# A convolution through DRAM in one step of a hybrid decoder: a smaller trip, the sample columns on VectorE, and the statistics moved into the next stage

## Chip, cores, metric

One Trainium2 chip, eight cores, every core running the same program on its share of the tokens. There is no exchange between cores. The metric is the device time of the slowest core in microseconds. Some executions fall into a second, slower state in which the cores of one die have a lower granted TensorE clock; times and ratios below use fast runs alone.

## The reference, cut to what matters

```python
def decoder_layer(x, ...):
    x = x + 0.5 * swiglu_ffn(rms_norm(x, ffn1_norm), ffn1_w_gu, ffn1_w_down)
    mix, v_state, conv_state = token_mixer(rms_norm(x, mix_norm), ...)
    x = x + mix
    return x + 0.5 * swiglu_ffn(rms_norm(x, ffn2_norm), ...), v_state, conv_state

def token_mixer(h, conv_prev, ...):
    ua, va, glu_a, glu_b, gate_a, gate_b = jnp.split(h @ w_in, SPLITS, axis=-1)
    u = jax.nn.gelu(ua)
    v = layer_norm(jax.nn.gelu(va), ln_v_g, ln_v_b)
    y_a = chunk_spatial_gating(u, v, w_s, b_s) @ w_pa      # u * (W_s v + b_s) per chunk of 128
    g = glu_a * jax.nn.sigmoid(glu_b)
    gpad = jnp.concatenate([conv_prev, g], axis=1)         # 30 earlier rows
    c = depthwise_conv(gpad, w_dw) + b_dw                  # width 31, 2048 channels
    y_b = jax.nn.silu(layer_norm(c, ln_c_g, ln_c_b)) @ w_pb
    m = jax.nn.sigmoid(gate_a) * y_a + jax.nn.sigmoid(gate_b) * y_b
    return m @ w_out, ...
```

Each core has 1024 prompt tokens, 64 sample tokens (16 sequences, 4 tokens each, with 30 cached rows) and 30 halo tokens before its prompt part: 1118 columns, channels on the partitions. The mixer runs as stages: V (for v), GLU with convolution (16 blocks of 128 channels), u (gelu, spatial gating, and beside it the layer norm and silu of the convolution), then gates and branch products.

## The kernel before

`P` is a planner: it records instructions per engine in the order of the Python calls and inserts a semaphore wait wherever a read or write depends on another engine. Each engine runs its list in the order in which it was recorded. `bank()` hands out the eight PSUM banks in turn. The depthwise convolution is a matmul: 32 channels by 4 shifts make the 128 rows, so the GLU result has to be laid out in four shifted copies, and for that it goes through DRAM (`gs_d`, "gspill").

```python
def glu(c):
    g = GBUF[c % 2]
    P.dma("pool", g[:, 1054:1534], cache_d[c])         # cached rows of the samples
    Wt = wk(W.get("glu", c), 256)
    for (c0, n) in S1:                                 # 374, 374, 370 columns
        ...                                            # 2 x 16 matmuls, sigmoid, product into g
    W.done("glu", c)                                   # slot free: starts the next 1 MB weight load
    P.dma("sp", gs_d[c % 2], g, wk=[("gs", c % 2)])    # the whole of g, 1614 columns
    P.dma("sp", gst_o[:, c, :], gf)
    g4 = G4R.get()
    for s in range(4):                                 # four shifts, prompt and samples apart
        P.dma("sp", g4[32*s:32*s+32, :, 0:GPN], src[:, :, s:s + GPN], rk=[("gs", c % 2)])
        P.dma("sp", g4[32*s:32*s+32, :, GPN:G4W], src[:, :, 1054+16*s:1054+16*s+GSN], rk=[("gs", c % 2)])
    ...
def conv(c, g4, dg):
    for (c0, n) in ((0, 512), (512, 512), (1024, 64)): # the third: the samples
        for q in range(8):
            for j in range(4):
                mm(bk[32*j:32*j+32, 0:n], dg[:, q, j, :], rhs, q == 0, q == 7)
        ...                                            # bias, square, running sums SM1, SM2

prev = glu(0)
v_norm()
for c in range(KC):
    nxt = glu(c + 1) if c + 1 < KC else None
    if c == 10:
        W.reserve(4); W.reserve(3)                     # slots kept for BSB and temporaries
    conv(c, *prev)
    prev = nxt
P.dma("sp", BSB..., bsr_d.to_broadcast([128, D]))      # bias table, in the last block's weight slot
...  # statistics of the convolution: 6 f32 matmuls, sqrt, reciprocal, three times in turn
...  # 4 matmuls and 16 VectorE operations that finish BSB
# [cut]
for c in range(KC):                                    # stage u
    for (c0, n) in SU:                                 # 384, 384, 320 columns
        ...                                            # 16 matmuls, 2 to 3 for the gating, gelu
        cn_step()                                      # one step of the convolution's layer norm
        if (c * 3 + SU.index((c0, n))) % 8 == 7:
            cn_step()                                  # subtract DVE, multiply POOL, 2 x ACT, product DVE
```

Of the kernel before, what the change touches and what calls it, by code (L numbers as in the profile page):

```python
# [25 lines left out]
SLOT_B = 8192  # L26
GW = 1054 + 544 + 16
GPN = 1052
GSN = 512
G4W = GPN + GSN  # L30

# [182 lines left out]
def build_program():  # L214
# [10 lines left out]
    pv_d = din("pv", [128, NVEC * 16])  # L225
    wcv_d = din("wcv", [128, 512])
    mask_d = din("mask32", [128, 32])
    maskt_d = din("maskt", [128, 128])
# [17 lines left out]
    xs_d = nc.dram_tensor("xspill", [KC, 128, NM], F32, kind="Internal").ap()  # L246
    gs_d = nc.dram_tensor("gspill", [2, 128, GW], BF16, kind="Internal").ap()

    P = Plan()
    with nc.sbuf_tensor("arena", [128, ARENA_B // 4], F32) as arena, \  # L250
# [78 lines left out]
        class Stream:  # L329
            def __init__(self):  # L330
                self.todo = []
                self.free = list(range(NSLOT))
                self.held = set()
                self.at = {}
                self.hold = {}

            def add(self, tiles):
                self.todo.extend(tiles)

            def pump(self):  # L340
                while self.todo:
                    tile = self.todo[0]
                    nm, i, allow = tile
                    pick = [s for s in self.free if s not in self.held and (allow is None or s in allow)]
                    if not pick:
                        return
                    s = pick[0]
                    self.free.remove(s)
                    self.todo.pop(0)
                    w = wd[nm].shape[2]  # L350
                    P.dma("pool", slots[s][:, 0:w], wd[nm][i], after=self.hold.pop((nm, i), ()))
                    self.at[(nm, i)] = s
# [196 lines left out]
        MV = view(o, [9, 2]); o += 72  # L549
        RS = view(o, [9]); o += 36  # L550
        NMR = view(o, [9]); o += 36
        WSTT = view(OFF_A + 32768, [16, 128])
# [45 lines left out]
        def v_norm():  # L598
            for (t, rows, c0) in vtiles:
                P.op("dve", lambda e, t=t, rows=rows: e.bn_aggr(  # L600
                    out=MV[0:rows, t, :], in_=ST[0:rows, t, :, :].rearrange("p a b -> p (a b)")),
                    [ST[0:rows, t, :, :]], [MV[0:rows, t, :]])
            for (r, a, b) in ((128, 0, 8), (64, 8, 9)):
                act(RS[0:r, a:b], MV[0:r, a:b, 1], AF.Sqrt, bias=EPSV[0:r, 0:1], scale=1.0)
                recip(RS[0:r, a:b], RS[0:r, a:b])
                stt(NMR[0:r, a:b], MV[0:r, a:b, 0], -1.0, RS[0:r, a:b], ALU.mult, ALU.mult)
            for vi, (t, rows, dst) in enumerate(((7, 128, vlast_o), (8, 64, vsamp_o))):
                vt = VT[vi]
                ts(vt[0:rows], V[0:rows, t, :], RS[0:rows, t:t + 1], NMR[0:rows, t:t + 1], ALU.mult, ALU.add)
                tt(vt[0:rows], vt[0:rows], LNG[0:rows], ALU.mult)  # L610
                tt(vt[0:rows], vt[0:rows], LNB[0:rows], ALU.add)
                P.dma("sp", dst, vt[0:rows])
            for (t, rows, c0) in vtiles:
                ts(V[0:rows, t, :], V[0:rows, t, :], RS[0:rows, t:t + 1], NMR[0:rows, t:t + 1], ALU.mult, ALU.add)

# [5 lines left out]
        GFR = ring(o, 2, [94]); o += 2 * 376  # L621
        assert o <= OFF_A + SZ_A
        o = OFF_T
# [4 lines left out]
        assert o <= ARENA_B  # L628

        def glu(c):  # L630
            g = GBUF[c % 2]
            if c < 2:
                memset(g[:, GW - 16:GW], 0.0)
            P.dma("pool", g[:, 1054:1534], cache_d[c])
            Wt = wk(W.get("glu", c), 256)
            gf = GFR.get()
            for (c0, n) in S1:
                ba, bb = bank(), bank()
                for k in range(KC):
                    mm(bb[:, 0:n], Wt[:, k, 128:256], H1[:, k, c0:c0 + n], k == 0, k == KC - 1)  # L640
                for k in range(KC):
                    mm(ba[:, 0:n], Wt[:, k, 0:128], H1[:, k, c0:c0 + n], k == 0, k == KC - 1)
                t = TSR.get()
                act(t[:, 0:n], bb[:, 0:n], AF.Sigmoid)
                for (a, b, dst) in ((0, NP_, 30), (NP_, NM, 1534), (NM, NT, 0)):
                    lo, hi = max(a, c0), min(b, c0 + n)
                    if lo < hi:
                        tt(g[:, dst + lo - a:dst + hi - a], t[:, lo - c0:hi - c0], ba[:, lo - c0:hi - c0], ALU.mult)
                if c0 + n == NT:
                    a = NM - 94 - c0  # L650
                    tt(gf, t[:, a:a + 94], ba[:, a:a + 94], ALU.mult)
            W.done("glu", c)
            P.dma("sp", gs_d[c % 2], g, wk=[("gs", c % 2)])
            P.dma("sp", gst_o[:, c, :], gf)
            g4 = G4R.get()
            src = gs_d[c % 2].rearrange("(j p) n -> p j n", p=32)
            for s in range(4):
                P.dma("sp", g4[32 * s:32 * s + 32, :, 0:GPN], src[:, :, s:s + GPN], rk=[("gs", c % 2)])
                P.dma("sp", g4[32 * s:32 * s + 32, :, GPN:G4W],
                      src[:, :, 1054 + 16 * s:1054 + 16 * s + GSN], rk=[("gs", c % 2)])  # L660
            dg = DGR.get()
            tt(dg.rearrange("p q j n -> p (q j) n"), MASK.unsqueeze(1).to_broadcast([128, 32, 32]),
               WCV[:, c, :].unsqueeze(2).to_broadcast([128, 32, 32]), ALU.mult)
            return g4, dg

        def conv(c, g4, dg):
            for (c0, n) in ((0, 512), (512, 512), (1024, 64)):
                bk = bank()
                for q in range(8):
                    for j in range(4):  # L670
                        rhs = (g4[:, j, 4 * q + c0:4 * q + c0 + n] if n == 512
                               else g4[:, j, GPN + 64 * q:GPN + 64 * q + 64])
                        mm(bk[32 * j:32 * j + 32, 0:n], dg[:, q, j, :], rhs, q == 0, q == 7)
                act(CN[:, c, c0:c0 + n], bk[:, 0:n], AF.Identity, bias=pv(PV_BDW, c), scale=1.0)
                if c == 0:
                    act(SM2[:, c0:c0 + n], bk[:, 0:n], AF.Square, bias=pv(PV_BDW, c), scale=1.0)
                else:
                    sq = SQC.get()
                    act(sq[:, 0:n], bk[:, 0:n], AF.Square, bias=pv(PV_BDW, c), scale=1.0)
                    tt(SM2[:, c0:c0 + n], SM2[:, c0:c0 + n], sq[:, 0:n], ALU.add)  # L680
            if c == 0:
                cp(SM1, CN[:, c, :])
# [4 lines left out]
        v_norm()  # L687
        for c in range(KC):
            nxt = glu(c + 1) if c + 1 < KC else None
            if c == 10:  # L690
                W.reserve(4)
                W.reserve(3)
            conv(c, *prev)
            prev = nxt

        US = view(OFF_A + KC * NM * 2, [KC, NM], BF16)
# [12 lines left out]

        sb_ = []  # L710
        for (c0, n) in S2:
            b1, b2 = bank(), bank()
            sb_.append((b1, b2))
            mm(b1[:, 0:n], ONESF, SM1[:, c0:c0 + n], True, True)
            mm(b2[:, 0:n], ONESF, SM2[:, c0:c0 + n], True, True)
        for (c0, n), (b1, b2) in zip(S2, sb_):
            ts(MEAN[:, c0:c0 + n], b1[:, 0:n], 1.0 / D, 0.0, ALU.mult, ALU.add)
            d = DR.get()
            stt(d[:, 0:n], MEAN[:, c0:c0 + n], -1.0, MEAN[:, c0:c0 + n], ALU.mult, ALU.mult)
            stt(RSC[:, c0:c0 + n], b2[:, 0:n], 1.0 / D, d[:, 0:n], ALU.mult, ALU.add)  # L720
            act(RSC[:, c0:c0 + n], RSC[:, c0:c0 + n], AF.Sqrt, bias=EPSV[:, 0:1], scale=1.0)
            recip(RSC[:, c0:c0 + n], RSC[:, c0:c0 + n])
        for q in range(4):
            bk = bank()
            mm(bk, ONESB, WST[:, 4 * q:4 * q + 4, :].rearrange("p a b -> p (a b)"), True, True)
            for hh in range(4):
                h = 4 * q + hh
                stt(BSB[:, h, :], bk[:, hh * 128:(hh + 1) * 128], pv(PV_LVB, h), BSB[:, h, :], ALU.mult, ALU.add)

        ts(PV[:, PV_LCG * 16:PV_LCG * 16 + 32], PV[:, PV_LCG * 16:PV_LCG * 16 + 32], 0.5, 0.0, ALU.mult, ALU.add)  # L730
        pend = {}
# [24 lines left out]
        def cn_step():  # L756
            i = step["i"]
            if i >= 2 and i - 2 < len(jobs):
                cn_c(*jobs[i - 2])
            if i >= 1 and i - 1 < len(jobs):  # L760
                cn_b(*jobs[i - 1])
            if i < len(jobs):
                cn_a(*jobs[i])
            step["i"] = i + 1

        for c in range(KC):
            Wt = wk(W.get("u", c // 2), 256)
            ci = c % 2
            for (c0, n) in SU:
                bk = bank()  # L770
# [19 lines left out]
                tt(US[:, c, c0:c0 + n], t1[:, 0:n], u[:, 0:n], ALU.mult)  # L790
                cn_step()
                if (c * 3 + SU.index((c0, n))) % 8 == 7:
                    cn_step()
            if ci == 1:
                W.done("u", c // 2)
# [249 lines left out]
```

## Time and profile before

| | before |
|---|---|
| fast runs | 3327 to 3338 us, and one of 3370 |
| TensorE waits, stages GLU to u, over five cores read | 46 to 56 us |
| of these on the trip through DRAM | 35 to 45 us |
| granted clock, mean of the span | 0.983 to 0.986 |

The page splits the span; the chain of waits follows the work that ended last. The prediction shows the lines for the bound. Three lines from the chain, for the first block; the columns are start, length and what it was, and for waits total us, times, longest:

```profile
1203.70 16.68 DMA arena<-cache
1220.46 9.91 DMA gspill<-arena
1233.26 13.98 DMA arena<-gspill
```

### The profile page before, as it was taken

The numbers are of one execution on the slowest core, as the hardware profiler recorded it, in microseconds if no ns is written. First come the engines' busy times: TensorE is split into PE (matmuls) and PEld (weight loads), VectorE is DVE, ScalarE is ACT, GpSimd is POOL, SyncE is SP. The second block draws the span as 40 slices with busy tenths as digits, with TensorE's granted clock in tenths as the row PEclk, the third lists the DMA queues.
The fourth block names the chain that finished last, engine by engine and source line by source line (L and its number), as shares of the span: only waits on it lengthen the run. The fifth ranks groups of instructions, "written<-read, shape, count | busy, mean of one in ns | idle before, by whom it ended". The sixth has DMA issues, their size and how long they took to land.

```text
span 3331.4 us, 50664 instructions; the slowest of 8 cores (3317.2 to 3331.4 us)
## 1 busy us (share of the span) xinstructions
PE 3182.9 (96%) x21149; PEld 1943.8 (58%) x21154; DVE 904.4 (27%) x1660; ACT 472.2 (14%) x910; POOL 180.1 (5%) x304
## 2 busy tenths in 40 slices
PE   5999999999998989997999999999999999999995
PEld 2666666666664445554666666665666666666653
DVE  4112112112126342223851111136112112112136
ACT  3000000000012112222640101012000000000011
POOL 0000000000000000000320000000000000000000
PEclk9999999999999999998999999999999999999997
DMA  7434334334335967774243334365435434435336
GB/s 178 83 55 85 70 55 85 70 56 85 69 63 119 206 124 148 154 158 104 52 91 64 75 77 77 73 174 102 76 54 93 72 54 85 73 59 92 64 59 158
DMA packets 80432, 307.31 MB, mean 92 GB/s; under 512 B 10000, under 2 KB 32784, under 8 KB 58640
## 3 DMA queue, kind: packets, MB, share of 16 engines
q0 software_dynamic: 36288, 225.53, 38.4%
q1 hardware_dynamic: 43920, 78.54, 8.8%
q8 instruction: 172, 2.82, 0.3%
q14 instruction: 52, 0.43, 0.0%
HBM read 502.77 MB, written 30.19 MB: 160 GB/s over the span
## 4 chain that ended last, share of the span: by engine, by line
PE 88%; DMA 6%; DVE 2%; SPq 1%; issue 1%; ACT 1%; DVEq 0%; POOL 0%; ACTq 0%; POOLq 0%
PE ps L299 88%; DMA gspill<-arena 2%; DMA arena<-gspill 2%; SPq L923 1%; DVE arena L318 1%; DMA arena<-w_v 1%; ACT arena L303 1%; DMA arena<-xin 1%; DVE arena L309 1%; DMA arena<-cache 1%; DVE arena L322 0%; POOL arena L923 0%; ACT L303 0%; DVEq L915 0%; DVE arena L313 0%
## 5 line engine op out<-in xcount | busy, mean ns | idle before, releaser
L299 PE MATMUL ps<-arena 128*128 128x364 bf16 (+11 forms) x21149 | 3182.9, 323 | 139.9 <-DMA arena<-gspill 45.0
L299 PEld LDWEIGHTS ps<-arena 128*128 128x128 bf16 (+2 forms) x21154 | 1943.8, 98 | 1378.7 <-issue 187.2
L309 DVE TENSOR_TENSOR arena<-arena,ps 128x374 bf16<-128x374 f32 (+7 forms) x456 | 223.6, 499 | 1707.2 <-PE ps L299 1706.9
L303 ACT ACTIVATE arena<-ps 128x364 f32<-128x364 f32 (+6 forms) x492 | 238.0, 484 | 2346.4 <-PE ps L299 2346.3
L318 DVE SCALAR_TENSOR_TENSOR arena<-ps,arena 128x364 f32<-128x364 f32 (+8 forms) x467 | 243.0, 526 | 351.7 <-PE ps L299 350.7
L309 DVE TENSOR_TENSOR arena<-arena 128x384 f32<-128x384 f32 (+14 forms) x361 | 229.6, 644 | 185.1 <-ACT arena L303 175.2
L303 ACT ACTIVATE arena<-arena 128x384 f32<-128x384 f32 (+9 forms) x293 | 162.8, 568 | 343.5 <-DVE arena L318 176.3
L318 DVE SCALAR_TENSOR_TENSOR arena<-arena 128x384 bf16<-128x384 f32 (+11 forms) x245 | 133.4, 589 | 3.4 <-ACT arena L303 1.9
L923 POOL DMA_DIRECT2D arena<-w_gu x88 | 46.8, 532 | 1067.9 <-PE ps L299 1008.1
L923 POOL DMA_DIRECT2D arena<-w_dn x73 | 38.7, 530 | 902.3 <-PE ps L299 902.3
L303 ACT ACTIVATE arena<-ps,arena 128x512 bf16<-128x512 f32 (+6 forms) x108 | 53.7, 563 | 125.5 <-PE ps L299 125.4
L309 POOL TENSOR_TENSOR arena<-arena 128x364 f32<-128x364 f32 (+1 forms) x48 | 45.8, 954 | 144.3 <-DVE arena L309 144.3
L322 DVE RECIPROCAL arena<-arena 128x384 f32<-128x384 f32 (+11 forms) x17 | 37.0, 2176 | 48.5 <-ACT arena L303 48.5
L580 DVE BATCH_NORM_STATS2 arena<-arena 128x6 f32<-128x512 bf16 (+1 forms) x36 | 24.8, 693 | 87.3 <-ACT arena L303 87.3
L309 DVE TENSOR_TENSOR arena<-ps,arena 128x384 f32<-128x384 f32 (+1 forms) x48 | 25.5, 530 | 28.7 <-DMA arena<-xspill 14.7
L923 POOL DMA_DIRECT2D arena<-w_gate x16 | 8.6, 535 | 398.1 <-PE ps L299 398.1
L303 ACT ACT_TABLE_LOAD x17 | 21.8, 1283 | 35.6 <-PE ps L299 14.3
L923 POOL DMA_DIRECT2D arena<-w_glu x16 | 8.5, 533 | 284.3 <-PE ps L299 284.3
L923 POOL DMA_DIRECT2D arena<-w_wo x11 | 5.8, 532 | 150.7 <-PE ps L299 150.7
L923 POOL DMA_DIRECT2D arena<-cache x16 | 8.9, 558 | 10.1 <-DMA gspill<-arena 9.9
L313 DVE TENSOR_SCALAR arena<-arena 128x2048 bf16<-128x2048 bf16 (+4 forms) x12 | 9.4, 837 | 0.0
L923 POOL DMA_DIRECT2D arena<-w_v x8 | 4.2, 536 | 95.0 <-PE ps L299 95.0
(10 smaller groups left out, 17.6 us busy)
## 6 DMA issues: line engine op xcount, KB each, us to landing
arena<-w_gu POOLq DMA_DIRECT2D x88, 1024.0 KB, 8.9
arena<-w_dn POOLq DMA_DIRECT2D x73, 704.0 KB, 6.6
arena<-gspill SPq DMA_DIRECT2D x64, 263.0 KB, 6.3
arena<-w_glu POOLq DMA_DIRECT2D x16, 1024.0 KB, 9.9
arena<-w_pab POOLq DMA_DIRECT2D x16, 1024.0 KB, 12.7
arena<-w_gate POOLq DMA_DIRECT2D x16, 1024.0 KB, 8.3
arena<-w_wo POOLq DMA_DIRECT2D x11, 1024.0 KB, 14.1
xspill<-arena SPq DMA_DIRECT2D x16, 544.0 KB, 28.8
```

The lines of the kernel that those rows point to most:

```text
L299: return P.op("pe", lambda e: e.matmul(out, lhsT, rhs, start=start, stop=stop), [lhsT, rhs], [out])
L303: return P.op("act", lambda e: e.activation(out=out, in_=in_, func=func, **kw), rd, [out])
L309: return P.op(eng, lambda e: e.tensor_tensor(out=out, in0=in0, in1=in1, op=op), [in0, in1], [out])
L313: return P.op("dve", lambda e: e.tensor_scalar(out=out, in0=in0, scalar1=s1, scalar2=s2, op0=op0, op1=op1), rd, [out])
L318: return P.op("dve", lambda e: e.scalar_tensor_tensor(out=out, in0=in0, scalar=s, in1=in1, op0=op0, op1=op1), rd, [out])
L322: return P.op("dve", lambda e: e.reciprocal(out=out, in_=in_), [in_], [out])
L580: P.op("dve", lambda e, t=t, rows=rows, pr=pr: e.bn_stats(out=ST[0:rows, t, pr, :], in_=V[0:rows, t, pr * 512:(pr + 1) * 512]), [V[0:rows, ...
L923: e.dma_start(out=item[1], in_=item[2]).then_inc(dsem[item[3]], 16)
```

## The change

The intent is to take TensorE's waits out of the loop and to fill the gap that the convolution's statistics leave behind it. The parts, in the numbers of the prediction: (1) the samples and the cache leave the DRAM trip, the store is cut into pieces sent as they are ready, four reads stand for eight, and weight loads are held until the reads have landed (`W.behind`); (2) the sample convolution becomes two products and two reductions on VectorE; (3) the last convolution and the statistics move into stage u, and the normalisation starts later, in more steps per segment. Also v's normalisation is spread over the first blocks.

```diff
@@ pump
-  P.dma("pool", slots[s][:, 0:w], wd[nm][i], after=self.hold.pop((nm, i), ()))
+  P.dma("pool", slots[s][:, 0:w], wd[nm][i], after=list(self.hold.pop((nm, i), ())) + self.behind)
@@ glu
-  P.dma("pool", g[:, 1054:1534], cache_d[c])
+  P.dma("pool", g[:, 1056:1536], cache_d[c])
-  for (c0, n) in S1:
+  for gi, (c0, n) in enumerate(GSEG):                  # S1[2], S1[0], S1[1]
+      if dst != 1536:
+          P.dma("sp", gs_d[c % 2][:, d0:d1], g[:, d0:d1], wk=[("gs", c % 2, d0)])
+      bgpop(2)                                         # v's normalisation, two pieces
-  P.dma("sp", gs_d[c % 2], g, wk=[("gs", c % 2)])
-  for s in range(4):  (two reads each)
+  W.behind = [P.dma("sp", g4[32*s:32*s+32, :, :], src[:, :, s:s + G4W], rk=[...]) for s in range(4)]
+  W.done("glu", c)
@@ conv
+  for i, (k0, k1) in enumerate(((0, 16), (16, 31))):   # samples on VectorE
+      tt(PRD[:, 0:k1-k0, :], win, WDW[:, c, k0:k1]..., ALU.mult)
+      tensor_reduce(out=ACC[i], in_=PRD[...].rearrange("p k n -> p n k"), op=add, axis=X)
+  stt(ACC[2], ACC[0], pv(PV_BDW, c), ACC[1], ALU.add, ALU.add)
-  for (c0, n) in ((0, 512), (512, 512), (1024, 64)):
+  for (c0, n) in ((0, 512), (512, 512)):
@@ loop
-  for c in range(KC):
-      nxt = glu(c + 1) if c + 1 < KC else None
+  for c in range(KC - 1):                              # the last conv() moves into u
+      nxt = glu(c + 1)
@@ cn_step: the subtraction of job i now stands before the product of job i - 2
@@ u
+  if i3 == 6: conv(KC - 1, *prev)
+  if i3 in (14, 20): recip(RSC[...])                   # second and third reciprocal
+  if i3 == 9: conv_stats(); conv_norm()
-  cn_step()
-  if i3 % 8 == 7: cn_step()
+  if i3 >= 10:
+      cn_step()
+      if i3 % 3 == 2: cn_step()
```

## The prediction

> **What bounds the kernel now.** The page comes first. TensorE is busy for nearly the whole span, and the chain of work that ended last is mostly TensorE.
>
> ```profile
> PE 3182.9 (96%) x21149; PEld 1943.8 (58%) x21154; DVE 904.4 (27%) x1660; ACT 472.2 (14%) x910; POOL 180.1 (5%) x304
> PE 88%; DMA 6%; DVE 2%; SPq 1%; issue 1%; ACT 1%; DVEq 0%; POOL 0%; ACTq 0%; POOLq 0%
> ```
>
> So a gain can only be TensorE idle time taken away, TensorE work taken away, or time at a reduced clock taken away. The span less TensorE's busy time is 148.5 us, and the change touches only the stages GLU/convolution (about 1202 to 1562 us) and u (1562 to 1712). The waits of TensorE tell how much of it lies there: first from 1190 to 1560, then from 1560 to 1900.
>
> ```profile
> PE ps L299 <- DMA arena<-gspill: 45.0, 9, 15.2
> PE ps L299 <- issue: 0.3, 1, 0.3
> ...
> PE ps L299 <- DVE arena L313: 4.5, 2, 4.3
> PE ps L299 <- DVE arena L309: 3.4, 1, 3.4
> PE ps L299 <- DVE arena L318: 2.6, 1, 2.6
> ```
>
> That is 45.3 + 10.5 = 55.8 us. The timeline of TensorE places it:
>
> ```profile
> 1247.69 40.48 PE L299 MATMUL ps<-arena 128*32 128x512 bf16 x384 [15.15 <-DMA arena<-gspill]
> 1291.14 19.19 PE L299 MATMUL ps<-arena 128*32 128x512 bf16 x192 [2.97 <-DMA arena<-gspill]
> ...
> 1437.06 38.50 PE L299 MATMUL ps<-arena 128*32 128x512 bf16 x384 [0.29 <-issue]
> ...
> 1556.56 5.23 PE L299 MATMUL ps<-arena 128*32 128x512 bf16 x96 [10.99 <-DMA arena<-gspill]
> 1565.19 6.45 PE L299 MATMUL ps<-arena 128*128 128x364 f32 x15 [3.40 <-DVE arena L309]
> ```
>
> One channel block is 192 instructions (96 GLU, 96 convolution), so 38.50 us is two blocks: 19.2 us each. The first wait is 15 us, the ones within the loop about 3 us, the last 11 us. The reason is in the chain: the GLU result is stored to DRAM and read back in shifted copies.
>
> ```profile
> 1457.15 10.03 DMA gspill<-arena
> 1469.99 7.49 DMA arena<-gspill
> 1542.66 3.59 DMA gspill<-arena
> 1549.04 7.07 DMA arena<-gspill
> ```
>
> The store takes 10.03 us in the loop, but 3.59 us the last time, when no weight load was started beside it. Loop latency: 0.8 us of VectorE after the block's end, 10.0 store, about 3 us of issues up to the last one (issues stand 0.47 us apart, eight of them), 7.5 to 8.7 for the last to land: 21.5 to 22.5 us, against the 19.2 us that the next convolution leaves it. That gives the 3 us waits.
>
> In the u stage TensorE never waits after 1586, but VectorE is nearly full (columns: length, then busy and count for PE, PEld, DVE, ACT, POOL):
>
> ```profile
> 1640.00:1660.00 20.00, 20.00 (x142) 12.86 (x141) 17.60 (x36) 14.53 (x25) 8.68 (x10) 1.00 0.48 88
> ```
>
> **What the Trainium skill says.** "TensorE: Matmul & The Clock Gate", section on the HAM clock gate, says that after an idle window of about 3.4 us the array runs at half clock until it has been busy about 3.4 us. The trace agrees (length, PE busy, clock, DMA):
>
> ```profile
> 1417.00:1437.00 20.00, 19.19 (x192) 1.00 0.79 163
> 1556.00:1562.00 6.00, 5.23 (x96) 0.72 0.35 138
> ```
>
> After the 11 us wait the granted clock is 0.72 and a convolution takes 5.23 us; within the loop it takes about 3.85. "DMA: Bandwidth & Descriptors", section "Issuing engines are not separate DMA queues", says that transfers of all issuing engines interleave on the same 16 DMA engines: 10.03 against 3.59 us for the same store agrees. "VectorE: DVE Perf Modes", tier table, says that tensor_reduce has only the 1x rate; no tensor_reduce is in this trace, so its cost below is an estimate.
>
> **The change, part by part.**
>
> 1. *Store in pieces, the last of 374 columns instead of 1614; the sample columns no longer go through DRAM; four reads instead of eight; weight loads held until the reads have landed.* The new latency, an estimate: 0.8 us VectorE + about 2.5 us store (below the 3.59 of the larger one) + 1.9 us of issues + 6 to 7 us landing = 11 to 13 us, inside the 18.8 us left. The weight load (9.9 us to landing) moves behind the reads, so it overlaps the next store by a few us at most. The waits in the loop go: 2.97 + 0.42 + 3.51 + 3.06 + 2.69 + 0.29 + 2.38 + 3.79 = 19.1 us. The first, 15.15 us, was a store held up by the cache load (16.7 us) and then by weights; the store no longer needs the cache. I leave 1 us of it, so 14.1 us is saved. Reduced clock after three of these waits: the runs of 384 took 40.48 and 40.00 where two blocks take 38.5, and the run of 288 took 25.53 where 23.1 is due: 2.0 + 1.5 + 2.4 = 6 us. Sum 39 us.
>
> 2. *The sample convolution moves from TensorE to VectorE.* 32 matmuls of 64 columns go. From ScalarE's first operation after the convolution's second bank (1440.80) to the first sigmoid of the next block (1443.72) is 2.92 us, of which 16 matmuls of 374 columns at 158 ns are 2.53: 0.4 us. Times 16: 6 us. VectorE gets two products of 1024 elements (1.22 us, from the 128x1024 group) and two reductions (estimate 1.2 us): 4.9 us per block, on top of about 6.3 us of work in 18.8 us. It fits.
>
> 3. *The last convolution, the statistics and the normalisation are moved into the u stage.* The end of the loop loses its waits: 11.0 + 3.4 + 4.5 + 2.6 = 21.5 us. Also reduced clock: the convolution 5.23 for 3.85, the first two u segments 7.5 for 5.5, and the stretch from 1586 about 2.4: together 6 us. Sum 27 us.
>
> 4. *What comes instead, at the start of u.* The bias table (the transfer from bsr) is still issued on SyncE behind the last block's store and reads, because its buffer is the last block's weight slot. Counting from that block's end: 0.8 VectorE, 2.5 store, 2.3 for four reads and the state output, so it is issued near 6 us and lands 9.1 us later (its time before), near 15. TensorE now arrives much sooner: convolution 3.45, four matmuls 0.9, two u segments 2 x 2.8, so at 10 us. The third u segment needs the first of the four banks that the bias table's matmuls hold; these are emptied only after landing and four VectorE operations of 0.27 us. Wait: 16.4 - 10 = 6.4 us, plus 1.7 us of reduced clock: 8 us back.
>
> 5. *What comes instead, in u.* Three segments take TensorE 2.82 + 2.82 + 2.34 = 8.0 us. The normalisation used 3.375 steps per three segments; now it starts at the eleventh segment and must use four. On VectorE three segments cost: gating 0.60 + 0.17 + 0.56, with 0.9 per step between starts, so about 2.3 us each with one step and 3.2 with two: 7.8 us, and a double step waits on ScalarE (in the trace it costs about 1 us more). The new order (subtract first) shortens that; I take 8.6. Excess 0.6 x 12.7 groups = 7.6, and two reciprocals of 2.43 us: 12.5 us. TensorE can run about 7.5 us ahead on eight banks, and VectorE is already some 2 us behind after the statistics: 7 us of waits. The lag left at the end holds up the first matmuls that need the gated result by about 3 us more, since only 4.9 us of gate matmuls lie before them. Together 10 us back.
>
> Sum: 39 + 6 + 27 - 8 - 10 = 54 us. The mean of the three fast runs is 3333.6, so 3279 us, 1.6% less.
>
> **Rivals.**
>
> (a) *The DRAM trip still binds.* Delayed weights collide with the next store and the waits stay near 3 us; the two bg stores of v do the same early on. For it: the DMA share is 0.7 to 0.8 in the loop. Against: the bytes fall, and the last store's 3.59 us. Then some 25 us less gain: about 3304.
>
> (b) *Nothing comes instead.* The normalisation chain runs at 7.8 us with the new order, and the bias table lands earlier. For it: the uneven segment numbers look tuned to the chip. Then the whole 72 us: 3262, just over 2%.
>
> (c) *VectorE becomes the bound of u.* Four steps take 9 us, as 2.4 + 2.4 + 4.2 us of the trace would say without the new order: 12 us more than a 8.0 us TensorE needs, on top of the reciprocals: 3285.
>
> **Range and chances.** The removed part is the better known, 72 us, give or take 6; the part that comes instead is 18, give or take 8. Range 3264 to 3296. 2% is 3266.9, which needs almost nothing to come instead: 0.22. Within 2%: 0.77. Slower: 0.01, as TensorE's work only shrinks.
>
> **What would show it.** Step 1: waits of TensorE on gspill under 3 us in all, and a block at about 18.8 us. Step 2: no 128x64 convolution matmuls, VectorE near 11 us a block. Step 3: no wait of 11 us before the statistics. Step 4: one wait of 5 to 8 us soon after the last block, released by a VectorE operation on the bias table. Step 5: waits of TensorE on VectorE of 5 to 15 us in the second half of u and at the first branch matmul. I am wrong if the gspill waits stay above 10 us, if step 4's wait is missing (then near 3270), or if u runs with more than 20 us of waits.

## More of the kernel before

```profile
SPq L917 <- DMA arena<-cache: 1.8, 1, 1.8
```

The store of the first block waits for the cache load, since the cached rows are part of what is stored, but only for 1.8 us: the block's own product ends at 1218.7. It is the only time that SyncE waits for a cache load; in the loop the store starts without it.

## The result

The changed kernel took 3281.4 us in the median of 11 runs (fast runs 3279.4 to 3282.3, the profiled one 3286.3), the kernel before 3337.0 in the median of 16, slow ones included in both. The ratio is 0.9834, 95% interval 0.9808 to 0.9861. The fast run of 3370 us is in it; without it the mean before is 3332.6, the changed kernel's is 3281.6, and the gain is 51 us. Ratios here are the mean time of one kernel's fast runs over that of the other's of the same rounds, so not quite the ratio of the quoted medians. The prediction was 3279, within 2%.

The page of after, busy times and the chain:

```profile
PE 3175.8 (97%) x20642; PEld 1934.8 (59%) x20642; DVE 998.0 (30%) x1740; ACT 471.3 (14%) x911; POOL 187.4 (6%) x304
PE 89%; DVE 4%; DMA 2%; issue 2%; ACT 1%; SPq 1%; POOL 0%; DVEq 0%; ACTq 0%; POOLq 0%
```

DMA has fallen from 6% to 2% of the chain, DVE has risen from 2% to 4%: the trip through DRAM is off the chain, and some of it came back as VectorE work. TensorE's waits of the slowest core, 1190 to 1530 us and then 1530 to 1900 us:

```profile
PE ps L298 <- DVE arena L317: 6.4, 1, 6.4
PE ps L298 <- DMA arena<-gspill: 3.4, 1, 3.4
PE ps L298 <- issue: 0.2, 1, 0.2
...
PE ps L298 <- ACT arena L302: 4.0, 5, 2.3
PE ps L298 <- DMA arena<-w_gate: 3.5, 1, 3.5
```

17.5 us, where the kernel before had 55.8: 38.3 us less. The timeline of TensorE places them:

```profile
1272.14 228.85 PE L298 MATMUL ps<-arena 128*32 128x512 bf16 x1920 [3.42 <-DMA arena<-gspill]
...
1517.77 71.98 PE L298 MATMUL ps<-arena 128*128 128x320 bf16 x513 [6.43 <-DVE arena L317]
1592.08 34.08 PE L298 MATMUL ps<-arena 128*128 128x384 bf16 x228 [2.34 <-ACT arena L302]
1626.56 8.22 PE L298 MATMUL ps<-arena 128*128 128x384 bf16 x57 [0.40 <-ACT arena L302]
...
1661.27 98.94 PE L298 MATMUL ps<-arena 128*128 128x364 bf16 x624 [3.47 <-DMA arena<-w_gate]
```

Twelve blocks of 160 matmuls now run without a break. The new waits are 6.43 us before the third u segment, 2.34 us in u, a 0.4 us wait that comes back every three segments (57 matmuls), and 3.47 us for the first gate weights. Other cores of the same run have the same waits in slightly other sizes: core 5 has 4.3, 5.2, 2.3 and, on gspill, 1.8 us.

The wait before the third u segment, in the timeline of all engines:

```profile
1506.16 0.43 SPq L964 DMA_DIRECT2D arena<-bsr  x1
...
1516.49 4.23 DVE L317 SCALAR_TENSOR_TENSOR arena<-ps,arena 128x128 f32<-128x128 f32 x16 [4.09 <-DMA arena<-bsr]
```

The bias table is issued 5.0 us after the last block's end (1501.2), lands 10.2 us later, and VectorE starts its 16 operations in the same moment. It is the wait of step 4, of the size that the prediction gave (6.4 us).

Windows of the slowest core (length; busy time and count of PE, PEld, DVE, ACT, POOL; granted clock; DMA share; GB/s) show what the two longer waits cost beyond themselves:

```profile
1517.00:1523.00 6.00, 5.23 (x21) 2.87 (x22) 5.65 (x20) 0.44 (x1) 0.00 (x0) 0.50 0.01 3
...
1661.00:1665.00 4.00, 3.73 (x13) 1.94 (x14) 3.54 (x8) 3.10 (x6) 1.64 (x2) 0.50 0.02 4
1665.00:1669.00 4.00, 4.00 (x21) 2.22 (x20) 0.94 (x2) 1.87 (x3) 1.05 (x2) 0.74 0.84 137
```

After the 6.43 us wait the clock is at half for 5.2 us of work, 2.6 us lost. After the 3.47 us wait it is at half for 3.7 us and at 0.74 for 4: 1.9 + 1.0 = 2.9 us lost. On core 5, where the same waits are 4.3 and 2.3 us, the second costs no clock.

The sum for the two profiled cores (core 2 before, core 0 after, the slowest of each): 38.3 us of waits, 4.6 us of sample matmuls (E1 below), and reduced clock. The latter was 12 us before by the prediction's count and is 9.5 us now: 2.6 and 2.9 as above, 2.8 in the twelve blocks (228.85 against 12 x 18.84, core 5's pace) and 1.2 in the stretch of 228 matmuls (34.08 against 4 x 8.22). That makes 38.3 + 4.6 + 2.5 = 45.4 us of the 46.7 us by which the span fell (3331.4 to 3284.7). In the prediction's terms about 66 us went (41.6 of waits on gspill, 10.5 of waits in the statistics, 4.6 of matmuls, 9.2 of reduced clock) where it had 72, and 20.6 us came (13.9 of waits, 6.7 of reduced clock) where it had 18.

### The profile page after: what moved, and what is told of

Read it like the earlier page. It is cut to its first block, busy times and chain, and to the rows that moved or that the text cites. A ratio compares the mean times of both kernels' runs of the same rounds, so it can differ in the third digit from the quotient of the medians.

```text
span 3284.7 us, 49921 instructions; the slowest of 8 cores (3272.8 to 3284.7 us)
## 1 busy us (share of the span) xinstructions
PE 3175.8 (97%) x20642; PEld 1934.8 (59%) x20642; DVE 998.0 (30%) x1740; ACT 471.3 (14%) x911; POOL 187.4 (6%) x304
## 4 chain that ended last, share of the span: by engine, by line
PE 89%; DVE 4%; DMA 2%; issue 2%; ACT 1%; SPq 1%; POOL 0%; DVEq 0%; ACTq 0%; POOLq 0%
PE ps L298 89%; DVE arena L317 3%; DVE arena L308 1%; ACT arena L302 1%; SPq L964 1%; DMA arena<-xin 1%; DMA gspill<-arena 0%; DVE arena L321 0%; POOL arena L308 0%; DMA arena<-bsr 0%; DMA arena<-w_gate 0%; DMA arena<-gspill 0%; DVEq L956 0%; ACT L302 0%; ACTq L956 0%
## 5 line engine op out<-in xcount | busy, mean ns | idle before, releaser
L298 PE MATMUL ps<-arena 128*128 128x374 bf16 (+6 forms) x20642 | 3175.8, 325 | 100.2 <-ACT arena L302 37.0
L298 PEld LDWEIGHTS ps<-arena 128*128 128x128 bf16 x20642 | 1934.8, 98 | 1341.0 <-issue 150.3
L317 DVE SCALAR_TENSOR_TENSOR arena<-ps,arena 128x384 f32<-128x384 f32 (+8 forms) x467 | 243.0, 526 | 354.4 <-PE ps L298 349.3
L308 DVE TENSOR_TENSOR arena<-arena 128x1024 f32<-128x1024 bf16 (+12 forms) x393 | 261.5, 686 | 122.4 <-ACT arena L302 107.0
L302 ACT ACTIVATE arena<-arena 128x384 f32<-128x384 f32 (+11 forms) x325 | 170.1, 535 | 394.1 <-DVE arena L317 227.3
L683 DVE TENSOR_REDUCE arena<-arena 128x64 f32<-128x1024 f32 (+1 forms) x32 | 59.9, 1873 | 3.3
L302 ACT ACTIVATE arena<-ps,arena 128x512 bf16<-128x512 f32 (+5 forms) x76 | 47.0, 666 | 81.5 <-PE ps L298 75.1
L308 POOL TENSOR_TENSOR arena<-arena 128x364 f32<-128x364 f32 (+1 forms) x48 | 53.4, 1113 | 74.6 <-DVE arena L308 74.6
```

What stands on the lines that cost most here:

```text
L298: return P.op("pe", lambda e: e.matmul(out, lhsT, rhs, start=start, stop=stop), [lhsT, rhs], [out])
L302: return P.op("act", lambda e: e.activation(out=out, in_=in_, func=func, **kw), rd, [out])
L308: return P.op(eng, lambda e: e.tensor_tensor(out=out, in0=in0, in1=in1, op=op), [in0, in1], [out])
L317: return P.op("dve", lambda e: e.scalar_tensor_tensor(out=out, in0=in0, scalar=s, in1=in1, op0=op0, op1=op1), rd, [out])
L683: P.op("dve", lambda e, src=src, dst=dst: e.tensor_reduce(out=dst, in_=src, op=ALU.add, axis=mybir.AxisListType.X), [src], [dst])
```

## The experiments

Twelve kernels ran, four at a time on one chip, each against the kernel before. All gave correct results. Means of fast runs: 

| run | what | us | ratio to before |
|---|---|---|---|
| control | the changed kernel again | 3283.1 (median) | 0.9886 |
| E1 | sample-sized matmuls added back | 3286.4 | 0.9861 |
| E2 | bias table earlier | 3278.0 | 0.9836 |
| E3 | gate weights first | 3277.9 (median) | 0.9862 |
| E4 | part 3 undone | 3292.0 | 0.9878 |
| E5 | no hold | 3284.4 | 0.9855 |
| E6 | one store, hold | 3279.6 | 0.9839 |
| E6b | one store, no hold | 3282.7 | 0.9848 |
| E7 | half of the double steps | 3271.2 | 0.9826 |
| E9 | E2, E3, E7 together | 3266.6 | 0.9812 |
| E10 | eight reads | 3284.5 | 0.9852 |
| E11 | v stores later | 3280.3 | 0.9841 |

The kernel before had means of 3332.6 (E1, E2, E4, E5), 3329.2 (control, E3, E7, E9) and 3334.2 us (the rest) in its fast runs, so 3 us between calls is not to be read; only one of the three calls has a control of its own. The control has one run of 3324.7 us and E3 one of 3293.6 that count as fast but stand apart (in the control's, cores of one die had 0.974 of the clock); for these two I give medians. Without that run the control's ratio would be about 0.986.

### Control

> The changed kernel itself, as a control on the chip of the next three: about 3281 us, ratio to before near 0.984.

Measured 3281.8 to 3283.9 us but for the one run, so the changed kernel takes 3281 to 3283 us.

### E1: what the sample convolution cost TensorE

```diff
             act(CN[:, c, NP_:NM], ACC[2], AF.Identity)      # before this line:
+            bk = bank()
+            for q in range(8):
+                for j in range(4):
+                    mm(bk[32*j:32*j+32, 0:64], dg[:, q, j, :], g4[:, j, 64*q:64*q+64], q == 0, q == 7)
```

> The changed kernel with 32 matmuls of 64 columns added back to each of the 16 convolutions (into a bank that nobody reads, so the result stays right). It measures what the sample convolution cost TensorE. By step 2 of the prediction 0.4 us a block: about 6 us slower than the changed kernel (3287). By the trace of after, where a block is 19.07 us against 19.25 before, only 0.2 us: about 3 us slower (3284).

TensorE's timeline of core 5, 13 unbroken blocks each; first the changed kernel, then E1:

```profile
1252.10 244.87 PE L298 MATMUL ps<-arena 128*32 128x512 bf16 x2080 [1.34 <-DMA arena<-gspill]
```

```profile
1252.57 248.63 PE L298 MATMUL ps<-arena 128*32 128x512 bf16 x2496 [1.67 <-DMA arena<-gspill]
```

18.84 against 19.13 us a block: 0.29 us for 32 matmuls of 64 columns, 4.6 us over 16 blocks, and 3.3 to 5.1 us in the time against the two readings of the changed kernel. The prediction's 6 us was a little high. My figure of 0.2 us in the expectation was read from core 0, whose stretch begins at half clock; it was the worse of the two. That is 9 ns a matmul. "TensorEngine Tiling (Array Packing)", section Key Properties, says that different tiles of the array can execute their matmuls in parallel; the matmuls here go to four tiles of 32 columns in turn, and the 9 ns agree with it.

### E2: the bias table earlier

```diff
-BSB = view(OFF_SLOTS + 4 * SLOT_B, [16, 128])       # slot of the last block's weights
+BSB = view(OFF_SLOTS + 3 * SLOT_B, [16, 128])       # slot of the last but one; DR, ZR move to slot 4
 for c in range(KC - 1):
+    if c == KC - 2:
+        P.dma("sp", BSB.rearrange("p a b -> p (a b)"), bsr_d.to_broadcast([128, D]))
     nxt = glu(c + 1)
```

> The changed kernel with the bias table in the slot of the last block but one and its transfer issued one block earlier, so that it has landed before TensorE gets to u. Theory (step 4): the 6.4 us wait before the third u segment goes, or shrinks to about 1 us (VectorE's backlog), and with it 1.7 us of reduced clock: 3273 to 3276. Rival: VectorE is the true limit at that point (it still has the convolution's sums to do) and the wait stays above 4 us: no change, 3281.

TensorE's waits on core 0:

```profile
PE ps L298 <- ACT arena L302: 5.2, 8, 2.4
PE ps L298 <- DVE arena L317: 2.5, 1, 2.5
```

The wait fell from 6.4 to 2.5 us (1.9 to 2.5 on the cores read), and the time by 3 to 5 us, less than expected. The rest is the rival's share, as the timeline shows:

```profile
1506.86 2.62 DVE L308 TENSOR_TENSOR arena<-arena 128x512 f32<-128x512 f32 x4
...
1509.40 4.22 DVE L317 SCALAR_TENSOR_TENSOR arena<-ps,arena 128x128 f32<-128x128 f32 x16
```

With the table there, its 16 operations start right behind the convolution's running sums, without a wait of VectorE. So of the 6.4 us about 4 were the late transfer and 2.5 are VectorE's backlog, for which both sample reductions stand before.

### E4: part 3 undone

```diff
-for c in range(KC - 1):
-    nxt = glu(c + 1)
+for c in range(KC):
+    nxt = glu(c + 1) if c + 1 < KC else None
+...  # statistics, sqrt and reciprocals before u, as in the kernel before
-if i3 == 6: conv(KC - 1, *prev)  (and the statistics at 9, reciprocals at 14 and 20)
-if i3 >= 10:
-    cn_step()
-    if i3 % 3 == 2: cn_step()
+cn_step()
+if i3 % 8 == 7: cn_step()
```

> The changed kernel with part 3 undone: the last convolution, the statistics and the inverse roots again stand before u, and the normalisation steps run from the first u segment as before. Prediction: part 3 is worth 27 us less 18 us of what comes instead, so this is about 9 us slower than the changed kernel (3290), with 8 to 11 us of waits on gspill and about 10 us of waits in the statistics. Rival: the new waits eat all of it: within 2 us of the changed kernel.

9 to 11 us slower than the changed kernel, by the two readings. TensorE's waits on core 5:

```profile
PE ps L298 <- DMA arena<-gspill: 11.5, 2, 9.1
PE ps L298 <- DVE arena L312: 4.5, 2, 4.3
PE ps L298 <- DVE arena L308: 3.7, 1, 3.7
PE ps L298 <- DVE arena L317: 2.6, 1, 2.6
```

They are the waits of the kernel before at the end of the loop, with 9.1 us for its 12.4 on this core, since the last block's trip is shorter (15.5 us before from the store's issue to the last landing, 11.5 here from the issue of the last piece). In the u stage TensorE then never waits. The net worth of part 3 is what the prediction said, 9 us.

### E5, E6, E6b, E10: which part of the DRAM trip counts

E5 takes the hold away:

```diff
-P.dma("pool", slots[s][:, 0:w], wd[nm][i], after=list(self.hold.pop((nm, i), ())) + self.behind)
+P.dma("pool", slots[s][:, 0:w], wd[nm][i], after=self.hold.pop((nm, i), ()))
```

> The changed kernel without holding weight loads behind the reads of gspill. Theory that the hold matters: store and reads run beside a weight load again, TensorE waits 1 to 3 us in most blocks, 15 to 30 us in all: 3295 to 3310. Rival: the smaller last store and four reads instead of eight are enough, waits on gspill stay under 5 us: 3281.

E6 stores once, at the block's end; E6b does both:

```diff
-            P.dma("sp", gs_d[c % 2][:, d0:d1], g[:, d0:d1], wk=[("gs", c % 2, d0)])   # in the segments
+    P.dma("sp", gs_d[c % 2], g[:, 0:1056], wk=[("gs", c % 2)])                        # after them
```

> The changed kernel with one store of 1056 columns at the block's end in place of the pieces; weights are still held. Store beside no weight load about 3.3 us: latency 0.8 + 3.3 + 1.9 + 6.5 = 12.5 us, far under 18.9: waits on gspill under 5 us, within 2 us of the changed kernel (3281 to 3283). Rival: the pieces are what counts, and waits of 1 us or more come back in most blocks.

> The same with the hold taken away too; what is left of the change to the DRAM trip is that the sample columns and the cache are out of it and that four reads stand for eight. Estimate from 10.0 us for 403 KB: store 6.7, so 0.8 + 6.7 + 1.9 + 7 to 8 = 16.4 to 17.4 us: mostly hidden, waits on gspill 5 to 10 us, 3284 to 3288. Rival: pieces or hold, one of the two is needed, and the waits are 15 us or more: over 3292.

E10 cuts each read in two:

```diff
-W.behind = [P.dma("sp", g4[32*s:32*s+32, :, :], src[:, :, s:s + G4W], ...) for s in range(4)]
+W.behind = [P.dma("sp", g4[32*s:32*s+32, :, a:a+526], src[:, :, s+a:s+a+526], ...)
+            for s in range(4) for a in (0, 526)]
```

> The changed kernel with each read cut into two halves of 526 columns, eight issues in place of four. Issue time rises by about 1.9 us, still hidden: within 2 us of the changed kernel, and the bias table is issued 1.9 us later, so its wait grows by 2 us: 3282 to 3284. Rival: the number of reads is what removed the waits: over 10 us of waits on gspill.

None of the four brought the waits back. On the four cores read, gspill cost TensorE 2.1 to 7.5 us in E5, at most 1.9 in E6, 1.0 to 5.0 in E6b and 0.5 to 4.8 in E10, against 35 to 45 in the kernel before. The times are 3279.6 to 3284.5 us. In E5, and on two cores in E6b, most of what is left is at the first convolution (1.4 to 5.8 us), where the changed kernel has no wait. In E10 the bias table is issued later, and its wait grew as expected, to 6.5 to 7.7 us. What the hold does is seen in the transfers of core 5 in 190 us of the loop (KB each, median us from issue to landing), before, after, E5 and E6b in this order:

```profile
arena<-gspill SPq DMA_DIRECT2D x38, 263.0 KB, 5.7
arena<-gspill SPq DMA_DIRECT2D x37, 128.0 KB, 5.8
gspill<-arena SPq DMA_DIRECT2D x9, 403.5 KB, 10.6
```

```profile
arena<-gspill SPq DMA_DIRECT2D x40, 263.0 KB, 4.9
gspill<-arena SPq DMA_DIRECT2D x21, 93.5 KB, 6.4
```

```profile
arena<-gspill SPq DMA_DIRECT2D x40, 263.0 KB, 9.1
gspill<-arena SPq DMA_DIRECT2D x21, 93.5 KB, 2.7
```

```profile
arena<-gspill SPq DMA_DIRECT2D x40, 263.0 KB, 7.7
gspill<-arena SPq DMA_DIRECT2D x10, 264.0 KB, 5.3
```

The weight load has to lie beside one half of the trip or the other: with the hold the stores are slow (6.4 us) and the reads fast (4.9), without it the other way round (2.7 and 9.1).

These medians mix the pieces of a block. What TensorE waits for is the whole trip, from the issue of a block's last store to the landing of its last read. Taken from the packed traces for the same 190 us, as medians of 9 to 11 blocks on cores 0, 2, 5 and 7:

| run | trip, us |
|---|---|
| before | 19.9 to 21.1 |
| changed kernel | 14.3 to 17.2 |
| changed kernel, control | 14.4 to 16.7 |
| E5, no hold | 14.6 to 15.9 |
| E6, one store | 14.5 to 16.7 |
| E6b, one store, no hold | 13.7 to 15.3 |
| E10, eight reads | 16.3 to 17.1 |

So neither the hold nor the pieces shorten the trip in the loop; E6b, without both, has the shortest. The waits in the loop were at most 3.8 us each on core 2 and 5.0 on core 5, and in E6b the trip is 5 to 7 us shorter, so taking the samples and the cache out of it, with four reads for eight, was enough there. E10 shows that the number of reads alone, with the rest of the change in place, doesn't decide it. The store's dependence on the cache load doesn't either, since it cost one wait of 1.8 us at the first block; what is left is the bytes (403 KB stored before, 264 now). That is by exclusion: no run puts the bytes back alone. Nor does a run undo the new order of the segments or the spreading of v's normalisation, which all four keep; the latter lies in the first blocks only.

### E3: the gate weights first

```diff
+W.add([("gate", 0, None), ("pab", 0, None)])
-for c in range(16):
+for c in range(1, 16):
     W.add([("pab", c, None), ("gate", c, None)])
```

> The changed kernel with the first gate weights loaded before the first branch weights (they are needed first). It asks what the 2 to 4 us wait for the gate weights at the end of u stands for. Theory of the prediction's step 5: VectorE ends u some 5 us behind TensorE, so without this wait TensorE meets a wait of about 3 us for the gated result instead: within 1 us of the control. Rival: only the late weights hold it up: 2 to 4 us faster, and no wait on VectorE there.

The median is 5.3 us below the control's (three runs 3276 to 3279, one 3293.6). TensorE's waits on core 5:

```profile
PE ps L298 <- DVE arena L317: 6.6, 1, 6.6
PE ps L298 <- ACT arena L302: 5.8, 9, 2.3
PE ps L298 <- DMA arena<-gspill: 2.3, 1, 2.3
```

The wait on the gate weights is gone and no wait of some 3 us on the gated result came in its place; ScalarE's waits grew by 0.6 us. So the rival was right, and the gain is above its 2 to 4 us. The cause of the late weights is read from the code and the timeline, not from a run that issues them elsewhere: it is their place in GpSimd's list. The load's buffer is free when TensorE finishes the 42nd u segment, but its issue stands behind GpSimd's multiplications of that segment, and those wait for VectorE. In the changed kernel TensorE ends that segment near 1640.4 us (two segments, 5.2 us, into the group of 57 matmuls that begins at 1635.15), but the timeline has the issue at 1652.0:

```profile
1651.96 0.59 POOL L964 DMA_DIRECT2D arena<-w_gate  x1
```

### E7: half of the double steps

```diff
-                    if i3 % 3 == 2:
+                    if i3 % 6 == 5:
```

> The changed kernel with every second double step of the normalisation dropped; about six steps are then left for after u. Theory: in u the loop VectorE, GpSimd, ScalarE needs 8.6 us per three segments with four steps against 8.2 us of TensorE; with 3.5 steps on average the repeated 0.4 us waits on ScalarE go, and the gate weights are issued earlier: 3 to 5 us faster. Rival: the six steps left over delay the first branch products by as much: no change or slower.

11.9 us faster than the control, more than twice what was expected. TensorE's waits on core 0:

```profile
PE ps L298 <- DVE arena L317: 5.6, 1, 5.6
PE ps L298 <- DMA arena<-gspill: 3.8, 3, 1.7
```

The waits on ScalarE (5.2 us in the control), the one on the gate weights (3.2 us there) are all gone, and with the latter the reduced clock that follows it (in the control 0.50 over the next 4 us and 0.74 over 4 more: 1.7 + 1.0 us). 5.2 + 3.2 + 2.7 = 11.1 us accounts for it. The five steps left for after u cost nothing that shows. So step 5's loop is confirmed as the cause: with four steps per three segments it was just over TensorE's pace. In the changed kernel's timeline three segments take it 8.6 us (VectorE's first gating operation of the group at 1642.54 and again at 1651.13):

```profile
1642.54 0.61 DVE L317 SCALAR_TENSOR_TENSOR arena<-ps,arena 128x384 f32<-128x384 f32 x1
...
1651.13 0.60 DVE L317 SCALAR_TENSOR_TENSOR arena<-ps,arena 128x384 f32<-128x384 f32 x1
```

### E9: the version that beats both

E2 and E3 and E7, with the bias table's four matmuls and 16 VectorE operations moved ahead of the second last convolution.

> A version meant to beat both: bias table loaded a block earlier and finished before the second last convolution, gate weights first, and half of the double steps. If the waits of steps 4 and 5 add up as predicted (6 + 2 + 4 + 3 us) it is 8 to 13 us faster than the control: 3268 to 3273. If one wait merely replaces another: 3276 or more.

3266.6 us in three fast runs (3264.1 to 3268.9), 16 us below the control, more than the 8 to 13 expected, and 0.9812 of the kernel before (interval 0.9795 to 0.9830, so that it can't be said whether it is 2% faster). TensorE's waits on core 0 in the three stages together:

```profile
PE ps L298 <- DMA arena<-gspill: 1.3, 1, 1.3
PE ps L298 <- ACT arena L302: 0.2, 1, 0.2
```

On cores 2, 5 and 7 it is 4 to 7 us in all, most of it on gspill. The waits of steps 4 and 5 added up and none took another's place.

### E11: the stores of v later

```diff
-                bg.append(lambda ...: P.dma("sp", dst, vt[0:rows]))      # blocks 1 and 2
+            ...  # 13 empty pieces, then the two stores, in blocks 5 and 6
```

> The changed kernel with the two stores of v (1 MB and 0.5 MB) issued in blocks 5 and 6 in place of 1 and 2. Theory (rival a of the prediction, in small): the one wait of 1 to 3 us on gspill early in the loop is due to them and goes, nothing comes later since the loop has slack by then: 0 to 3 us faster. Rival: the early wait is due to the weight loads of the first blocks and stays.

3280.3 us. On the four cores read gspill still costs 0 to 3.3 us, in the changed kernel 1.4 to 3.4. Inconclusive: two of the four cores lost the early wait, one kept it, and the time is within the spread.

## Why the prediction was right, point by point

**Step 1** had the size right and the reason partly wrong. It counted 33 us of waits saved (19.1 in the loop, 14.1 at the first block); on core 2 gspill fell from 45.0 us (34 without the last) to 1.4. It put the first wait down to the cache load and then to weights; the cache load delayed that store by 1.8 us only. The new latency was mis-sized: 11 to 13 us predicted, with 2.5 us for the last store. In the timeline of core 0 in the 15th block the last store is issued at 1482.89 and the reads only follow at 1490.92, 8 us later:

```profile
1482.89 0.32 SPq L964 DMA_DIRECT2D gspill<-arena  x1
...
1490.92 1.93 SPq L964 DMA_DIRECT2D arena<-gspill  x4
```

The statement that failed is that the weight load "overlaps the next store by a few us at most": the last store takes 7.0 to 9.3 us in the median of the four cores. With the 0.8 us of VectorE the latency is 15 to 18 us, just under the 18.8 left. The working also counts on the hold and the pieces; E5, E6 and E6b show that the loop needs neither.

**Step 2** said 6 us; E1 gives 4.6. VectorE bore it with 11.9 us of work a block ("near 11" was said), though tensor_reduce took 1.94 and 1.81 us instead of 1.2; these 1.35 us are part of the backlog in E2.

**Step 3**, net of steps 4 and 5, said 9 us; E4 gives 9 to 11.

**Step 4** said a wait of 6.4 us; core 0 has 6.43, the other cores read 3.7 to 6.2, so the match to the tenth is luck. Its working was right in the order but not in each term: issue at 5.0 us instead of 6, landing after 10.2 instead of 9.1. It left VectorE's backlog of 2.5 us out, because the transfer hid it. The reduced clock was 2.6 us and not 1.7.

**Step 5** said 10 us; core 0 has 4.0 + 3.5 + 2.9 of half clock = 10.4. The loop of 8.6 us per three segments was as worked out. Two things in it were wrong. TensorE's waits there (the sign was 5 to 15 us on VectorE; none came) are released by ScalarE, whose gelu stands behind the normalisation's activations in its queue, and not by VectorE. And the last 3 us are not a wait for the gated result: it is the gate weights, issued late by GpSimd for the same lag (E3). The sum came out right in part by luck: no reduced clock was counted here. One term also moved without being foreseen: GpSimd's multiplication takes 1.11 us where it took 0.95 before, and VectorE's subtraction 0.68 for 0.53; no run tests why.

**The rivals.** (a) did not come, but for 1 to 3 us early in the loop. (b), nothing comes instead, is wrong for the kernel as changed and is nearly what E9 does with 3266.6. (c) took the right cause too far. The whole came out closer (3281 against 3279) than its parts: about 6 us less went and 2.6 us more came than predicted in the profiled pair, whose second run (3286.3 us) is the slowest fast one of the changed kernel's first call.

## What to carry to other kernels

When a store and a read-back lie beside a steady load, moving the load can just move the contention from one to the other, as here; the trip got shorter with the bytes that were taken out of it. Work that fills a gap must leave every engine under the pace of the one that sets it: four steps per three segments were 8.6 us against 8.2 and cost 12 us, three and a half cost nothing. And look in which engine's in-order queue a transfer stands, since a load issued by GpSimd behind arithmetic that lags comes as late as the arithmetic.

## What the Trainium skill lacked or had wrong

- "VectorE: DVE Perf Modes", the tier table, has tensor_reduce at the 1x rate, without a time. A reduction of 128x1024 f32 to 128x64, read with a step of 64 elements, takes 1944 ns and one of 128x960 takes 1808 ns: (1944 - 1808) / 64 = 2.1 ns an element, half the rate of the f32 tensor_tensor with 1219 ns for 1024. The runs don't tell whether the step or the operation does it. The page has no figure for it:

```profile
L683 DVE TENSOR_REDUCE arena<-arena 128x64 f32<-128x960 f32 x12 | 21.7, 1808 | 1.2
L683 DVE TENSOR_REDUCE arena<-arena 128x64 f32<-128x1024 f32 x11 | 21.4, 1944 | 1.1
```

- "TensorE: Matmul & The Clock Gate", the section on the HAM clock gate, says to expect 13/16 of the clock once three cores of a die run dense matmuls. With all eight cores at it, each core's mean clock was 0.987 to 0.990 in nearly all fast runs of the changed kernel. Two runs that count as fast had less on one die (0.974 in the control's of 3324.7 us, 0.984 in E3's of 3293.6). In the slow runs, most of them on one die, it was 0.81 (E7's of 3899.2 us) to 0.96; the other die of such a run stayed at its usual figure. So the page's 13/16 is the lowest that came, and not the rule here.
- The same page's idle window of about 3.4 us is no sharp bound in a trace: half clock (0.50) followed waits of 3.42, 3.47 and 6.43 us on core 0 of the changed kernel, but there also one of 2.34 us (0.58 in the 4 us after it), while core 5 kept full clock after 2.37 us. That agrees with the page's remark that the window runs freely, and a wait of 2 to 3.4 us may or may not cost clock.
- No page that I read spells out that an engine behind in its arithmetic delays the weight loads that stand in its list: the buffer was free near 1640, GpSimd issued the load at 1652.
